# Two-layer RG-LRU and RWKV-7 decoder trunk on one core: a chunked scan with 64x64 products on all four quarters of the PE array, and smaller edits around it

## The chip, the core and the metric

The kernel runs on one core of a Trainium2 chip. The core has a matrix engine (TensorE, PE in the profile; PEld is its loading of stationary operands), a vector engine (VectorE, DVE), a scalar engine (ScalarE, ACT), a general engine (GpSimd, POOL) and a queue that issues most transfers (SyncE, SP). Each engine works through its own list of instructions in order and waits on semaphores for the others. The metric is the device time of one execution in microseconds (us).

## The reference, cut to what matters

The trunk has two layers on 1024 tokens of width 1024. Each layer is a token mixer (layer 0: RG-LRU; layer 1: RWKV-7), a cross-attention with 4 heads into 256 memory tokens, and a squared-ReLU MLP of width 4096. Every part is wrapped in two RMS norms, `x = x + rms_norm(f(rms_norm(x, g0)), g1)`. The part that the change rewrites is the recurrence of RWKV-7, for 16 heads of 64 channels:

```python
def step(state, inp):                     # state: 16 heads of 64 x 64
    r_t, w_t, k_t, v_t, a_t, b_t = inp
    sa = jnp.einsum('bhij,bhj->bhi', state, a_t)
    state = (state * w_t[:, :, None, :] + sa[..., None] * b_t[:, :, None, :]
             + v_t[..., None] * k_t[:, :, None, :])
    y_t = jnp.einsum('bhij,bhj->bhi', state, r_t)
    return state, y_t
_, ys = lax.scan(step, state0, seq_inputs)   # 1024 steps
```

Behind it each head's output is normalised over its 64 channels (mean and variance), scaled, shifted and gated.

## The kernel before

All large products run as three passes (`mm3`, lines 318 to 320): each 32-bit operand is split into a rounded part and a rest (`split`, line 233 on ACT and 234 on DVE). A recording pass lists all weight tiles, and a second pass loads and splits them ahead of use. The framework's scheduler may reorder instructions; `self.line(name)` keeps everything inside it in program order on each engine, and `self.behind()` keeps what it holds behind all that was issued.

**The scan** (lines 1657 to 1870) is cut into 16 chunks of 64 tokens; chunk c needs the state that chunk c-1 left. The 16 heads are 8 pairs (index q) of two heads (h), one on partitions 0 to 63 and one on 64 to 127 (`hr[h]`). Within a chunk, in the names of the code:

- `scan_gram(c, g)` (L1685): for half g of the heads, products of the chunk's keys `st` with its queries and removal vectors `mv`; `scan_mask` (L1695, DVE) masks them into `gw`, and ACT copies a block of `mv` beside it (L1697).
- `values(m)` (L1796): `gw` times the tile `sv`, which holds the state and the chunk's values; ACT copies the result (L1798). `from_state(m)` (L1808) is the state's share of the output. `solved(m)` (L1814) applies a triangular inverse; DVE scales the result and writes it into `sv` over the state (L1816).
- `decayed(m)` (L1803, POOL): the state times the chunk's total decay. It reads the state in `sv`, so L1816 of the same chunk has to wait for it.
- `scan_scale` (L1674, POOL) multiplies the keys with the chunk's decay; `scan_keys` (L1709, PE) transposes them, ACT copies them to `gk` (L1710).
- `update(m)` (L1821): `gk` times `sv`; DVE adds the decayed state (L1823), which is the state of the next chunk. `output()` (L1828) completes the chunk's output, which ACT copies (L1830).
- `post_var(c)` (L1721 on ACT: eight squares with sums; L1723 and L1724 on POOL: scale, then the power -1/2), `post_norm(c)` (L1729, DVE) and `flip_out(c)` (L1736 on PE, L1741 on DVE, L1742 on POOL) normalise, transpose and gate an earlier chunk's output.

The list `todo` sets the order of these in a chunk, all of it inside `self.line("scan")`. In chunk c the grams, masks, scaled and transposed keys of chunk c+1 are made. Before, `todo` reads: decayed, scan_scale(c+1), values and from_state by halves, **post_var(c-1)**, solved, flip_out(c-2), scan_gram(c+1, 0), update, scan_keys(c+1), scan_mask, scan_gram, scan_mask, output, post_norm(c-1). The loads of two chunks (`load`, L1630 for `st`, L1633 for `mv`) are issued on SP one pair of chunks ahead.

**Around the scan**: `tail` normalises the result of each part tile by tile (128 tokens): sum of squares on ACT (L327), scale and power on POOL (L329, L331), then on DVE result x norm x gain (L677) and + x (L678). `tphase` is the product before it, with the split of its first tile ahead of it. `xattn` goes through (head, half) steps: scores, softmax, transposes, values. `mlp` streams the up projection's results through memory, and its down projection begins with `block(0)`, `weights(0)`, `block(1)`.

## Time and profile before

| | |
|---|---|
| runs (3) | median 2851.32 us, 2850.32 to 2852.19 |
| profiled execution | 2850.88 us, span 2849.2 us, granted PE clock 0.993 |
| PE busy | 97% of the span |
| DVE, ACT, POOL busy | 65%, 50%, 32% |
| scan, chunks 2 to 14 (first product to first product of chunk 15) | 1764.38 to 1892.24 us |

The profile gives busy time by engine, groups of instructions by source line, waits with what ended them, and a timeline. In a timeline row the columns are start (us), length (us), engine, line, operation, output<-input tiles with their kinds (u, z: on-chip tiles, q, p: matmul banks, s, g: small columns, d: memory), shapes, and the count; a bracket gives the engine's idle time before the row and what ended it. A product of plain 32-bit operands is two PE instructions in the trace, a transpose one. Rows merge instructions that follow each other; a row's length runs to the end of the last one, which overlaps the next row's start.

### The profile page before, as it was taken

The numbers are of one execution on the slowest core, as the hardware profiler recorded it, in microseconds if no ns is written. First come the engines' busy times: TensorE is split into PE (matmuls) and PEld (weight loads), VectorE is DVE, ScalarE is ACT, GpSimd is POOL, SyncE is SP. The second block draws the span as 40 slices with busy tenths as digits, with TensorE's granted clock in tenths as the row PEclk, the third lists the DMA queues.
The fourth block names the chain that finished last, engine by engine and source line by source line (L and its number), as shares of the span: only waits on it lengthen the run. The fifth ranks groups of instructions, "written<-read, shape, count | busy, mean of one in ns | idle before, by whom it ended". The sixth has DMA issues, their size and how long they took to land.

```text
span 2849.2 us, 42748 instructions
## 1 busy us (share of the span) xinstructions
PE 2770.1 (97%) x16955; PEld 2312.1 (81%) x16955; DVE 1855.0 (65%) x2016; ACT 1424.0 (50%) x2191; POOL 912.2 (32%) x962
## 2 busy tenths in 40 slices
PE   7999999999999999999999999999999999999998
PEld 6888788888888888887777788888888888888886
DVE  5477557557454577888685835775665645567778
ACT  5456345545545544337672544654563644455333
POOL 2000114013666510003088223853203376640001
PEclk9999999999999999999999999999999999999999
DMA  8212342323454564424557799962222345464453
GB/s 264 74 45 77 101 165 83 104 82 100 152 161 148 204 211 155 155 89 134 171 150 225 215 252 241 240 155 96 78 86 97 99 160 159 148 240 162 149 176 118
DMA packets 383912, 421.92 MB, mean 148 GB/s; under 512 B 91504, under 2 KB 294496, under 8 KB 383712
## 3 DMA queue, kind: packets, MB, share of 16 engines
q1 hardware_dynamic: 371680, 379.19, 44.1%
q0 software_dynamic: 11568, 39.41, 3.8%
q8 instruction: 133, 2.18, 0.3%
q14 instruction: 67, 0.55, 0.1%
q10 hardware_dynamic: 464, 0.59, 0.1%
HBM read 283.79 MB, written 134.74 MB: 147 GB/s over the span
## 4 chain that ended last, share of the span: by engine, by line
PE 80%; POOL 5%; DVE 4%; DMA 3%; issue 3%; ACT 3%; SPq 2%; POOLq 0%; DVEq 0%; ACTq 0%
PE q L318 17%; PE q L320 17%; PE q L319 17%; PE p L318 7%; PE p L320 7%; PE p L319 7%; DMA u<-d 2%; POOL u L1434 2%; POOL w L1432 2%; PE q L1685 1%; ACT u L233 1%; DVE u L234 1%; POOL s L331 1%; PE q L1808 1%; DMA u<-in_b_w_rkv 1%
## 5 line engine op out<-in xcount | busy, mean ns | idle before, releaser
L234 DVE TENSOR_TENSOR u<-u,u 128x1024 fp32r<-128x1024 f32 (+1 forms) x602 | 808.5, 1374 | 351.7 <-ACT u L233 327.9
L233 ACT CAST u<-u 128x1024 fp32r<-128x1024 f32 (+1 forms) x602 | 591.5, 1019 | 443.0 <-DVE u L1064 224.6
L318 PE MATMUL q<-u,u 128*128 128x512 f32 (+1 forms) x1952 | 744.1, 383 | 5.7 <-ACT u L233 2.4
L319 PE MATMUL q<-u,u 128*128 128x512 f32 (+1 forms) x1952 | 745.6, 382 | 0.0
L320 PE MATMUL q<-u,u 128*128 128x512 f32 (+1 forms) x1952 | 740.6, 382 | 0.8 <-DVE u L234 0.8
L318 PE MATMUL p<-u,u 128*128 128x512 f32 (+1 forms) x1472 | 555.1, 379 | 17.3 <-ACT u L233 7.2
L320 PE MATMUL p<-u,u 128*128 128x512 f32 (+1 forms) x1472 | 552.4, 375 | 4.9 <-DVE u L234 4.9
L319 PE MATMUL p<-u,u 128*128 128x512 f32 (+1 forms) x1472 | 553.1, 376 | 2.4 <-DVE u L234 2.3
L329 POOL TENSOR_SCALAR s<-s 128x1 f32<-128x1 f32 x98 | 40.8, 417 | 1268.3 <-ACT u L327 1266.6
L318 PEld LDWEIGHTS q<-u,u 128*128 128x128 f32 x1952 | 367.0, 188 | 78.5 <-ACT u L233 3.5
L320 PEld LDWEIGHTS q<-u,u 128*128 128x128 f32 x1952 | 366.8, 188 | 72.1 <-DVE u L234 1.0
L319 PEld LDWEIGHTS q<-u,u 128*128 128x128 f32 x1952 | 367.1, 188 | 70.3 <-DVE u L234 0.3
L318 PEld LDWEIGHTS p<-u,u 128*128 128x128 f32 x1472 | 280.8, 191 | 70.5 <-ACT u L233 12.8
L320 PEld LDWEIGHTS p<-u,u 128*128 128x128 f32 x1472 | 280.9, 191 | 56.9 <-DVE u L234 7.5
L319 PEld LDWEIGHTS p<-u,u 128*128 128x128 f32 x1472 | 281.2, 191 | 52.8 <-DVE u L234 5.0
L444 POOL TENSOR_TENSOR u<-u,u 128x512 f32<-128x512 f32 x120 | 186.1, 1556 | 8.9 <-PE q L319 5.1
L1122 DVE TENSOR_TENSOR z<-z,q 128x512 f32<-128x512 f32 x192 | 130.5, 683 | 80.9 <-PE q L320 80.9
L318 PE MATMUL q<-z,u 128*128 128x512 f32 x320 | 124.9, 390 | 1.6 <-ACT u L233 1.6
L319 PE MATMUL q<-z,u 128*128 128x512 f32 x320 | 124.5, 389 | 0.0
L320 PE MATMUL q<-z,u 128*128 128x512 f32 x320 | 124.2, 389 | 0.0
L445 POOL TENSOR_TENSOR u<-u 128x512 f32<-128x512 f32 x40 | 75.9, 1897 | 145.4 <-DVE u L234 73.1
L1019 POOL TENSOR_TENSOR u<-u,u 128x512 f32<-128x512 f32 x32 | 46.0, 1436 | 176.6 <-ACT u L1008 166.7
(251 smaller groups left out, 3317.2 us busy)
## 6 DMA issues: line engine op xcount, KB each, us to landing
u<-d SPq DMA_DIRECT2D x194, 512.0 KB, 4.8
d<-u SPq DMA_DIRECT2D x109, 512.0 KB, 3.3
d<-u POOLq DMA_DIRECT2D x68, 512.0 KB, 3.3
d<-u SPq DMA_DIRECT2D x132, 256.0 KB, 3.4
u<-in_m_w_up SPq DMA_DIRECT2D x64, 512.0 KB, 5.4
u<-in_m_w_down SPq DMA_DIRECT2D x64, 512.0 KB, 7.5
u<-in_c_w_kv SPq DMA_DIRECT2D x32, 512.0 KB, 6.5
u<-in_b_w_rkv SPq DMA_DIRECT2D x24, 512.0 KB, 6.6
```

What stands on the lines that cost most here:

```text
L233: self.nc.scalar.copy(hv, src)
L234: (eng or self.nc.vector).tensor_tensor(lv, src, hv, ALU.subtract)
L318: mm(o, ah, bh, start=first, stop=False, **kw)
L319: mm(o, ah, bl, start=False, stop=False, **kw)
L320: mm(o, al, bh, start=False, stop=last, **kw)
L329: nc.gpsimd.tensor_scalar(v, ss, 1.0 / n, eps, ALU.mult, ALU.add)
L444: sub = lambda o, x, y: nc.gpsimd.tensor_tensor(o, x, y, ALU.subtract)
L445: nc.gpsimd.tensor_tensor(s[:, a], f1[:, a], f1[:, b], ALU.add)
L1019: tt(s1, r21, r22, ALU.add)
L1122: nc.vector.tensor_add(to_, to_, o)
L1432: eng.tensor_tensor(tv, xv_[:, 0:n, s:s + 1].broadcast_to([128, n, m]), Lv[:, s:s + 1, s + 1:].broadcast_to([128, n, m]), ALU.mult)
L1434: eng.tensor_tensor(xv_[:, 0:n, s + 1:], xv_[:, 0:n, s + 1:], tv, ALU.add)
```

## The change

In the scan, `scan_gram`, `from_state`, `solved` and the keys are written as products on 64 x 64 quarters of the array that go round all four quarters (`quads`, `tile_position`), with the heads of the upper half of q stored swapped. The keys are no longer scaled by POOL and transposed; POOL makes a diagonal tile (identity x decay, one 128x512 instruction for two), and one product with it scales and transposes at once. `st` is loaded in runs of 128 tokens for 64. The output bank is one per half of the heads. `todo` has a new order, in which `post_var(c-1)` is last in the chunk and `post_norm` is one chunk later. Outside the scan: `tail` multiplies result and gain ahead of the norm and joins the rest in one DVE instruction; the last tile's norm has fewer POOL steps; `tphase` can split its first tile in two cuts and does so behind RG-LRU; the last GELU is in two halves; `xattn` has another order of its steps, loads an activation table earlier and moves the held sums; `mlp` issues `block(1)` later.

```diff
-    def tphase(self, rows, z, post, mid=None):
+    def tphase(self, rows, z, post, mid=None, cuts=1):
 
         zs = {}
 
         def zsplit(tt):
             if tt < 8:
-                zs[tt] = self.split(z(tt), view=lambda t: t.rearrange("p (k t) -> p k t", t=128))
+                zs[tt] = self.unit(F32R), self.unit(F32R)
+                n = KT // (1 if tt else cuts)
+                for k in range(0, KT, n):
+                    self.split(z(tt)[:, k:k + n], *zs[tt], view=lambda t: t.rearrange("p (k t) -> p k t", t=128)[:, k:k + n])
 
...
-        def first(tt, src, ss):
+        def first(tt, src, r):
+            if r is None:
+                r = self.rstd(src, self.unit())
             o = self.unit()
-            r = self.rstd(src, o, ss=ss)
+            for s in (slice(512, 1024), slice(0, 512)) if last and tt >= HALVES else (slice(0, 1024),):
+                nc.vector.tensor_mul(o[:, s], src[:, s], gb[:, s])
             for n in range(1 + FETCH[last]):
                 fetch(tt + n)
             x = held[tt]
@@ -669,13 +674,10 @@
 
                     for n in range(2):
                         s = slice(n * 512, n * 512 + 512)
-                        y = self.unit()
-                        nc.vector.scalar_tensor_tensor(y[:, s], src[:, s], r, gb[:, s], ALU.mult, ALU.mult)
-                        nc.vector.tensor_add(y[:, s], y[:, s], x[:, s])
-                        (nc.sync, nc.scalar)[n].dma_start(xdst[tt * 128:tt * 128 + 128, s], y[:, s])
+                        nc.vector.scalar_tensor_tensor(o[:, s], o[:, s], r, x[:, s], ALU.mult, ALU.add)
+                        (nc.sync, nc.scalar)[n].dma_start(xdst[tt * 128:tt * 128 + 128, s], o[:, s])
                     return
-                nc.vector.scalar_tensor_tensor(o, src, r, gb, ALU.mult, ALU.mult)
-                nc.vector.tensor_add(x, o, x)
+                nc.vector.scalar_tensor_tensor(x, o, r, x, ALU.mult, ALU.add)
...
+            nc.scalar.activation(self.small(1), self.nhalf[:, :1], AF.Exp)
+            held, self.held = self.held, None
+            with self.behind(), self.line("held"):
...
-        steps = [(hd, hf) for hd in range(4) for hf in range(2)]
+        steps = [(0, 0), (0, 1), (1, 0), (1, 1), (2, 0), (3, 0), (2, 1), (3, 1)]
...
             block(0)
             weights(0)
+
+        def first():
             block(1)
-
-        def first():
             for work in parts(0):
...
-                        nc.gpsimd.tensor_tensor(sq[0], sq[0], sq[1], ALU.add)
-                        post(7, acc[1][:, 3, :], sq[0])
+                        nc.gpsimd.tensor_scalar(sq[0], sq[1], 1.0 / D, sq[0], ALU.mult, ALU.add)
+                        nc.gpsimd.tensor_tensor(sq[1], sq[0], self.nhalf[:, :1], ALU.pow)
+                        post(7, acc[1][:, 3, :], sq[1])
...
-            st = self.unit().rearrange("p (e q w t) -> p e q w t", e=2, q=4, w=2)
-            for e in range(2):
-                es = slice(n * 128 + e * 64, n * 128 + e * 64 + 64)
-                nc.sync.dma_start(st[:, e], STd[:, 4 * g:4 * g + 4, :, es])
+            st = self.unit().rearrange("p (q w t) -> p q w t", q=4, w=2)
+            nc.sync.dma_start(st, STd[:, 4 * g:4 * g + 4, :, ts])
...
+    quads = [(0, 0), (1, 1), (0, 1), (1, 0)]
+
     def scan_scale(c):
 
         if c >= 15:
             return
         s = cst[c]
-        s["sc"] = self.unit()
-        scv = s["sc"].rearrange("p (q w t) -> p q w t", q=8, w=2)
-        for g in range(2):
-            qs = slice(4 * g, 4 * g + 4)
-            nc.gpsimd.tensor_tensor(scv[:, qs], s["st"][g], s["pcc"][:, qs].unsqueeze(3).broadcast_to([128, 4, 2, 64]), ALU.mult)
+        s["sc"] = self.unit()[:, 0:512].rearrange("p (q i) -> p q i", i=64)
+        nc.gpsimd.tensor_tensor(s["sc"], self.id64.unsqueeze(1).broadcast_to([128, 8, 64]),
+                                s["pcc"].broadcast_to([128, 8, 64]), ALU.mult)
 
...
-            for h in range(2):
+            for h, w in quads:
                 with self.line("gram"):
-                    mm(s["pv", g][h][:, q, :], s["st"][g][hr[h], q].rearrange("p w t -> p (w t)"), s["mv"][hr[h], 4 * g + q],
-                       start=True, stop=True)
+                    mm(s["pv", g][h][hr[w], q, :], s["st"][g][hr[h], q, w, :], s["mv"][hr[h], 4 * g + q],
+                       start=True, stop=True, tile_position=(h * 64, w * 64))
 
...
+        s["gk"] = self.unit().rearrange("p (q h i) -> p q h i", q=8, h=2)
+        tps = [self.bank(h).rearrange("p (q i) -> p q i", i=64) for h in range(2)]
+        for q in range(8):
+            for h, w in quads:
+                mm(tps[h][hr[w], q, :], s["st"][q // 4][hr[h], q % 4, w, :], s["sc"][hr[h], q, :],
+                   start=True, stop=True, tile_position=(h * 64, w * 64))
+        for h in range(2):
+            nc.scalar.copy(s["gk"][:, :, h, :], tps[h])
...
+        def from_state():
+            Y.extend(self.bank(m)[:, 0:256].rearrange("p (q i) -> p q i", i=64) for m in range(2))
+            for q in range(4):
+                for h, m in quads:
+                    mm(Y[m][hr[h ^ m], q, :], mv[hr[h], m * 4 + q, 1, :], sv[hr[h], m * 4 + q, h, :],
+                       start=q == 0, stop=False, tile_position=(h * 64, (h ^ m) * 64))
+
+        def solved():
+            for q in range(4):
+                for h, m in quads:
+                    r = h ^ m
+                    mm(U[m][hr[h], q, :], xtc[hr[r], m * 4 + q, :], wsb[m][hr[r], q, :], start=True, stop=True,
+                       tile_position=(r * 64, h * 64))
+            for m in range(2):
+                qs = slice(m * 4, m * 4 + 4)
+                for h in range(2):
+                    nc.vector.tensor_tensor(sv[hr[h], qs, h, :], U[m][hr[h]], dbv[hr[h], qs].broadcast_to([64, 4, 64]), ALU.mult)
 
...
+        more = c and c < 15
         todo = [(decayed, 0), (decayed, 1)] if c < 15 else []
-        if c:
+        if more:
             todo += [(scan_scale, c + 1)]
-        todo += [(values, 0), (from_state, 0), (values, 1), (from_state, 1)]
-        if c:
-            todo += [(post_var, c - 1)]
-        todo += [(solved, 0), (solved, 1)]
+        todo += [(values, 0), (values, 1), (from_state,)]
+        if more:
+            todo += [(scan_gram, c + 1, 0)]
+        todo += [(solved,)]
+        if more:
+            todo += [(scan_keys, c + 1)]
+        if c < 15:
+            todo += [(update, 0), (update, 1)]
+        if more:
+            todo += [(scan_mask, c + 1, 0), (scan_gram, c + 1, 1)]
+        todo += [(output,)]
+        if c > 1:
+            todo += [(post_norm, c - 2)]
+        if more:
+            todo += [(scan_mask, c + 1, 1)]
         if c > 1:
             todo += [(flip_out, c - 2)]
         if c:
-            todo += [(scan_gram, c + 1, 0)]
-        if c < 15:
-            todo += [(update, 0), (update, 1)]
-        if c:
-            todo += [(scan_keys, c + 1, 0), (scan_keys, c + 1, 1), (scan_mask, c + 1, 0), (scan_gram, c + 1, 1), (scan_mask, c + 1, 1)]
-        todo += [(output,)]
-        if c:
-            todo += [(post_norm, c - 1)]
+            todo += [(post_var, c - 1)]
...
```

In the listings of the built programs that follow, names are output<-inputs, with buffer numbers: u and g are on-chip tiles, z the queries and removal vectors, pc the decays, id the 64 x 64 identity. First POOL in the scan before, one chunk from its decayed states on (L1803: decayed, L1674: scaled keys, L1723 and L1724: variance and power of chunk c-1, L1742: gate of an earlier chunk), and the start of the next:

```order
L1803 TENSOR_TENSOR u_16077<-u_16083,pc 64x256 x4
L1674 TENSOR_TENSOR u_16614<-u_16422,pc 128x512
L1674 TENSOR_TENSOR u_16614<-u_16425,pc 128x512
L1723 TENSOR_SCALAR g_16653<-g_16653 128x8
L1724 TENSOR_TENSOR g_16653<-g_16653,nhalf 128x8
L1742 TENSOR_TENSOR u_16524<-u_16524,u_15734 128x8x64
L1803 TENSOR_TENSOR u_16430<-u_16433,pc 64x256 x4
```

The same place on POOL now (L1818: decayed, L1688: the diagonal, L1759: gate, L1740 and L1741: variance and power of chunk c-1):

```order
L1818 TENSOR_TENSOR u_15249<-u_15255,pc 64x256 x4
L1688 TENSOR_TENSOR u_15906<-id_8762,pc 128x512
L1759 TENSOR_TENSOR u_15887<-u_15887,u_14829 128x8x64
L1740 TENSOR_SCALAR g_16095<-g_16095 128x8
L1741 TENSOR_TENSOR g_16095<-g_16095,nhalf 128x8
L1818 TENSOR_TENSOR u_15682<-u_15685,pc 64x256 x4
```

Variance and power stood between the scaled keys and the gate; now they stand behind the gate, directly ahead of the next chunk's decayed states.

ACT in the scan before, one chunk from the copies of `values` on (L1798), with the squares of chunk c-1 (L1721), the copies of the keys (L1710), those beside the masks (L1697) and that of the output (L1830):

```order
L1798 COPY u_15549<-q_15558 128x256
L1798 COPY u_15549<-q_15576 128x256
L1721 ACTIVATE u_15384,g_15594<-u_15384 128x64 x8
L1710 COPY u_15662<-q_15663 128x512
L1710 COPY u_15662<-q_15669 128x512
L1697 COPY u_15675<-z_13697 64x4x64 x2
L1697 COPY u_15690<-z_13697 64x4x64 x2
L1830 COPY u_15549<-q_15550 128x512
L1798 COPY u_15737<-q_15746 128x256
```

ACT now (L1813: values, L1727: keys, L1712: beside the masks, L1850: the output by halves, L1738: squares of chunk c-1):

```order
L1813 COPY u_15901<-q_15908 128x256
L1813 COPY u_15901<-q_15918 128x256
L1727 COPY u_15984<-q_15985 128x8x64
L1727 COPY u_15984<-q_15986 128x8x64
L1712 COPY u_16041<-z_13731 64x4x64 x2
L1850 COPY u_15901<-q_15928 128x256
L1850 COPY u_15901<-q_15929 128x256
L1712 COPY u_16083<-z_13731 64x4x64 x2
L1738 ACTIVATE u_15695,g_16095<-u_15695 128x64 x8
L1813 COPY u_16128<-q_16135 128x256
L1813 COPY u_16128<-q_16145 128x256
```

The squares stood right behind the copies of `values`; now they stand behind the last copy that follows the masks, ahead of the next chunk's copies of `values`.

DVE in the scan before, from the scaling of `solved` (L1816) on: gate product of an earlier chunk (L1741), the sums that make the next state (L1823), masks (L1695), norm (L1729):

```order
L1816 TENSOR_TENSOR u_15021<-q_15393,db 64x256 x2
L1816 TENSOR_TENSOR u_15021<-q_15411,db 64x256 x2
L1741 TENSOR_TENSOR u_15465<-q_15460,u_14677 128x8x64
L1823 TENSOR_TENSOR u_15024<-u_15018,q_15393 64x256 x2
L1823 TENSOR_TENSOR u_15024<-u_15018,q_15411 64x256 x2
L1695 TENSOR_TENSOR u_15511<-q_15468,mask 128x4x128
L1695 TENSOR_TENSOR u_15511<-q_15469,mask 128x4x128
L1695 TENSOR_TENSOR u_15526<-q_15516,mask 128x4x128
L1695 TENSOR_TENSOR u_15526<-q_15517,mask 128x4x128
L1729 TENSOR_TENSOR u_15196<-u_15196,g_15429 128x512
```

DVE now (L1837: scaling, L1844: sums, L1710: masks, L1746: norm, L1758: gate product):

```order
L1837 TENSOR_TENSOR u_15255<-q_15918,db 64x256
L1837 TENSOR_TENSOR u_15255<-q_15908,db 64x256 x2
L1837 TENSOR_TENSOR u_15255<-q_15918,db 64x256
L1844 TENSOR_TENSOR u_15685<-u_15249,q_15908 64x256 x2
L1844 TENSOR_TENSOR u_15685<-u_15249,q_15918 64x256 x2
L1710 TENSOR_TENSOR u_16041<-q_15946,mask 128x4x128
L1710 TENSOR_TENSOR u_16041<-q_15947,mask 128x4x128
L1746 TENSOR_TENSOR u_15468<-u_15468,g_15890 128x512
L1710 TENSOR_TENSOR u_16083<-q_16046,mask 128x4x128
L1710 TENSOR_TENSOR u_16083<-q_16047,mask 128x4x128
```

The gate product moved from between scaling and sums to the chunk's end, and the norm from behind the four masks to between them.

76 lines of the change are left out of this document (33 added, 43 removed).

## The prediction

> **What bounds the kernel now.** I read the page first: busy shares and the chain that ended last.
>
> ```profile
> span 2849.2 us, 42748 instructions
> ...
> PE 2770.1 (97%) x16955; PEld 2312.1 (81%) x16955; DVE 1855.0 (65%) x2016; ACT 1424.0 (50%) x2191; POOL 912.2 (32%) x962
> ...
> PE 80%; POOL 5%; DVE 4%; DMA 3%; issue 3%; ACT 3%; SPq 2%; POOLq 0%; DVEq 0%; ACTq 0%
> ```
>
> PE is busy for 97% of the span and carries 80% of the chain. So an edit pays where it shortens PE's own work or one of the few waits in front of PE, and costs where it makes PE wait. Most of the diff lies in the scan, so I asked for the busy time of each engine between the first `values` product of chunk 2 and that of chunk 15, which is 13 chunks.
>
> ```profile
> core 0: us, PE busy (x) PEld busy (x) DVE busy (x) ACT busy (x) POOL busy (x), PEclk, DMA share, GB/s
> 1764.38:1892.24 127.86, 125.55 (x2644) 111.85 (x2644) 93.73 (x181) 74.94 (x320) 95.80 (x110) 0.99 0.97 223
> ```
>
> A chunk takes 127.86 / 13 = 9.84 us, with PE busy 98% and the transfers' engines 0.97 (the column before the last). POOL is busy 75% of it, DVE 73%. The timeline of one chunk shows how that closes:
>
> ```profile
> 1809.69 1.15 PE L1821 MATMUL q<-u,u 128*64 128x64 f32 x32
> 1810.42 1.77 DVE L1823 TENSOR_TENSOR u<-u,q 64x256 f32<-64x256 f32 x4 [0.15 <-PE q L1821]
> ...
> 1810.77 1.09 PE L1709 MATMUL q<-ident,u 128*128 128x128 f32 x8
> ...
> 1811.80 1.16 PE L1685 MATMUL q<-z,u 64*128 64x128 f32 x16
> 1812.22 2.66 POOL L1803 TENSOR_TENSOR u<-u,pc 64x256 f32<-64x256 f32 x4
> 1812.22 2.48 DVE L1695 TENSOR_TENSOR u<-q,mask 128x512 f32<-128x512 f32 x4
> ...
> 1814.63 0.80 DVE L1729 TENSOR_TENSOR u<-u,g 128x512 f32<-128x512 f32 x1
> 1814.74 0.40 ACT L1697 COPY u<-z 64x256 f32<-64x256 f32 x1 [0.19 <-DVE u L1695]
> 1814.95 2.37 POOL L1674 TENSOR_TENSOR u<-u,pc 128x512 f32<-128x512 f32 x2
> ...
> 1815.65 0.68 ACT L1798 COPY u<-q 128x256 f32<-128x256 f32 x2
> ...
> 1815.84 0.68 PE L1808 MATMUL q<-u,z 64*64 64x64 f32 x16
> ...
> 1816.35 0.26 ACT L1721 ACTIVATE u<-u 128x64 f32<-128x64 f32 x1
> 1816.35 1.33 PE L1814 MATMUL q<-u,u 64*64 64x64 f32 x32
> ...
> 1817.13 1.78 DVE L1816 TENSOR_TENSOR u<-q,db 64x256 f32<-64x256 f32 x4 [1.70 <-PE q L1814]
> ...
> 1818.18 0.19 ACT L1721 ACTIVATION_READ_ACCUMULATOR u<-u 128x1 f32 x1
> ...
> 1818.45 0.20 POOL L1723 TENSOR_SCALAR g<-g 128x8 f32<-128x8 f32 x1 [1.13 <-ACT u L1721]
> 1818.73 1.65 POOL L1724 TENSOR_TENSOR g<-g,nhalf 128x8 f32<-128x8 f32 x1
> ...
> 1820.35 1.28 POOL L1742 TENSOR_TENSOR u<-u,u 128x512 f32<-128x512 f32 x1
> ```
>
> Three things are to be seen. PE goes from one block to the next. The decayed states (POOL L1803) start at 1812.22, as soon as the sums that make the state end (DVE L1823, 1810.42 + 1.77 = 1812.19). And the squares of an earlier chunk (ACT L1721), its variance and its power (POOL L1723, L1724: 1818.45 to 1820.35) run while PE does other work; before the next state is ready only the gate (L1742) follows them on POOL. In these rows nobody waits for POOL.
>
> **The scan, step by step.** *PE's own work.* 32 instructions that use two quarters at a time take 1.08 us (L1821 starts 1809.69, the next block 1810.77), 34 ns each. What four quarters give is shown by the gram products of an earlier stage, of the same 64x64x64 shape, which already go round all four:
>
> ```profile
> 1381.68 1.16 PE L1403 MATMUL q<-u,u 64*64 64x64 f32 x64
> 1382.78 0.96 PE L1333 MATMUL q<-u,u 64*128 64x512 f32 x6
> ```
>
> 64 instructions in 1.10 us, 17.2 ns each. So `from_state` and `solved`, 32 instructions each, fall from 34 to 17.2 ns: -1.08 us a chunk. The keys become 64 instructions, 1.10 us, in place of 8 transposes, 1.03 us (1810.77 to 1811.80): +0.07. The gram stays: twice the instructions at half the time. PE would save 1.0 us a chunk. The Trainium skill (TensorEngine Tiling (Array Packing), Instruction Overhead) gives each matmul some 60 cycles of overhead, which at the 2.4 GHz of its front page (Trainium Kernel Development and Optimization, NeuronCore Architecture) is 25 ns, an estimate; read as a floor of one instruction it would make the keys 1.6 us and the forecast 6 us longer. The 17.2 ns are against that reading.
>
> *The order.* This decides. In the listings `post_var(c-1)` is now the last item of a chunk, on ACT behind the copies that follow the last masks, on POOL directly ahead of the next chunk's decayed states. Each engine works in order, so these states now wait for the power, the power for the squares, the squares for the masks, and the masks for the state. On the other side, L1837 may not overwrite the state before it was read, and the keys' product waits for the diagonal, which POOL makes behind the decayed states, while `update` stands behind the keys on PE. That closes a loop from one state to the next, and each of its parts has a row above:
>
> - two masks, norm, two masks on DVE: from 1812.22 to the end of L1729, 1815.43: 3.2 us;
> - the last copy beside a mask, from the last mask's end (1814.70) to 1815.14: 0.45;
> - eight squares and their sums, from 1816.35 until POOL starts on them at 1818.45: 2.1;
> - variance and power, until the next POOL instruction can start at 1820.35: 1.9;
> - four decayed states, 1812.22 to the scaling's start at 1814.95: 2.73;
> - the diagonal: one instruction of 128x512 for L1674's two, half of 2.37: 1.2. Both operands are now repeated along an axis, which no row shows; I bound it by one 64x256 instruction (2.66 / 4 = 0.67) and by both old ones (2.37), and take 1.2, as the size is the same;
> - PE's wait on POOL, 0.1 (an estimate from DVE's 0.15 on PE in the row of 1810.42), and the keys, 1.1 (bounds: 1.03 as now, 2.2 if only two quarters overlap);
> - `update` to the end of the sums, 1809.69 to 1812.19: 2.5.
>
> The sum is 15.3 us for a chunk, against 9.84. What could be longer lies inside: DVE's scaling of `solved` (1.78) waits for the third decayed state only, some 2 us after the first starts, and ends before the keys do; the copies of `values` (0.68) and `solved` run beside the power and the decayed states; `flip_out` runs beside the squares; grams and `output` fit into PE's idle time. The transfers have 5 us more per chunk, and fewer packets, as each run of `st` is twice as long.
>
> *How often.* `decayed` of chunk c stands behind `post_var` from chunk 2 on, to chunk 14. So the loop runs from the `update` of chunk 1 to that of chunk 14:
>
> ```profile
> 1757.92 1.17 PE L1821 MATMUL q<-u,u 128*64 128x64 f32 x32
> ...
> 1888.48 1.15 PE L1821 MATMUL q<-u,u 128*64 128x64 f32 x32
> ...
> 1897.53 2.04 PE L1828 MATMUL q<-u,u 128*64 128x64 f32 x32
> 1899.50 0.50 PE L318 MATMUL p<-u,u 128*128 128x512 f32 x1
> ```
>
> Before, that is 1888.48 - 1757.92 = 130.6 us. Now it is 12 x 15.3 and, for chunk 14, which makes no keys (no diagonal; `update` follows the scaling), 15.3 less 1.2, 1.1 and 0.1 and plus about 1.0 that the scaling then sticks out: 13.9; together 197.5. That is +66.9. Behind it, from the `update` of chunk 14 to the next product phase: before 1899.50 - 1888.48 = 11.0; now 2.5 + 3.2 + 0.45 + 2.0 (squares ahead of the copies of `values`) + 0.7 + 0.7 (`solved`) + 1.9 + 1.1 (`output`) = 12.6: +1.6. Chunks 0 and 1 may save 1 us each on PE; I count nothing there. Scan: **+68.5 us**. Bounds of the loop: 14.5 with the short diagonal, 17.6 with the long one and the keys by halves.
>
> **Outside the scan** PE's waits are the price list (the bracket is the idle time before the row):
>
> ```profile
> 304.35 0.50 PE L318 MATMUL p<-u,u 128*128 128x512 f32 x1 [3.06 <-ACT u L233]
> ...
> 532.28 1.28 ACT L952 ACT_TABLE_LOAD   x1 [1.86 <-DVE s L947]
> ...
> 535.56 0.39 PE L318 MATMUL p<-u,u 128*128 128x256 f32 x1 [2.07 <-ACT u L952]
> ...
> 579.03 1.14 PE L964 MATMUL q<-ident,u 128*128 128x128 f32 x8 [1.37 <-ACT z L977]
> ...
> 685.54 1.64 PE L390 MATMUL q<-ident,u 128*128 128x128 f32 x13 [0.66 <-DVE u L685]
> ...
> 965.75 0.50 PE L318 MATMUL q<-u,u 128*128 128x512 f32 x1 [1.18 <-ACT u L233]
> ...
> 2839.94 0.29 POOL L1132 TENSOR_TENSOR s<-s,s 128x1 f32<-128x1 f32 x1 [1.08 <-ACT u L1131]
> ...
> 2840.32 0.58 POOL L329 TENSOR_SCALAR s<-s 128x1 f32<-128x1 f32 x1
> ...
> 2842.62 0.68 DVE L674 TENSOR_TENSOR u<-u,u 128x512 f32<-128x512 f32 x1
> ...
> 2843.88 1.89 DVE L674 TENSOR_TENSOR u<-u,u 128x512 f32<-128x512 f32 x3
> ```
>
> RG-LRU's output product waits 3.06 for the split behind the last GELU; with two cuts the first half needs older tiles only: -2.5 (bounds -3.1 and 0). The scores wait 2.07, in which ACT loads a table for 1.28; loaded earlier: -1.3 (0 to -2.1). The new order of steps may remove waits such as the 1.37 or make others: -1 (+3 to -4). At three seams the transposes wait some 0.66 for a norm that loses one DVE instruction of about 1.2: -1.8 (0 to -2.0). The MLP's first cast waits 1.18 in each of two layers, and the later `block(1)` may free it a tile: -1.2 (0 to -2.4). At the end the four DVE instructions from 1841.95 on lose two of 0.6 to 0.7, and POOL's first two become one (0.29): -1.6 (-0.7 to -2.2). The moved sums of the attention: 0 (1.5 either way). Together **-9.4**, from +3.8 to -17.3 if all went one way.
>
> **The sum.** The profiled execution took 2850.88 us, 0.44 under the median of the runs (2851.32). 2850.88 + 68.5 - 9.4 = **2910 us**, 2% slower.
>
> **Rivals.**
>
> *PE stays the bound (faster).* If the loop took less than PE's work, a chunk would fall by the 1.0 us above: 13 x 1.0 and 9.4 less, 2828 us. For it speaks that PE is 98% busy now. By the Trainium skill (TensorEngine Tiling (Array Packing), Theoretical Speedup) a side of 64 or less gains up to twice in PE's throughput, which is this rival's mechanism. Against it: the loop would have to lose over 6 us, more than squares, variance and power together (4.0), and its links stand in program order. It decides only below about 8.8 us a loop. Chance 0.07.
>
> *The loop closes one step earlier.* If the diagonal of the next chunk were ready when `update` comes, the loop would end over the scaling, as in chunk 14: 13.9 for 15.3, so 2910 - 12 x 1.4 = 2893. The listing speaks against it: the diagonal stands behind the decayed states. Chance 0.12.
>
> *The quarters do not overlap* with operands cut out of longer rows: keys 2.2, +1.1 in the loop, 2910 + 13 = 2923. The gram would double too, but in PE's idle time. The 17.2 ns row speaks against it. Chance 0.1.
>
> *The edits outside the scan carry and the loop is hidden in part*, so that both cancel to within 0.2% (5.7 us, about what this measurement can tell from no change): the loop would be near 10.5 us. Chance 0.02.
>
> **Numbers.** The forecast has 0.69. The range reaches from 2880 (the shorter loop of the second rival with 13 us more saved outside or in shorter POOL instructions) to 2936 (the long diagonal, 12 x 1.2 = 14, and half of the keys' 13, with nothing saved outside beyond 4). Slower by over 0.2%: 0.91; within 0.2%: 0.02; faster: 0.07.
>
> **What would show it.** In the scan the starts of `update` 15.3 us apart; PE busy some 57% there (8.7 of 15.3); PE's wait in front of the keys (L1724), ended by POOL (L1688), some 4 us long and once in a chunk; POOL's squares-variance-power-decayed-diagonal without a gap; DVE's scaling (L1837) released by POOL (L1818). `from_state`, `solved` and keys at 17 ns an instruction. Outside: no wait of 3 us at RG-LRU's output product, PE's busy time down by about 13 x 1.0. It is wrong if POOL's power no longer takes 1.65, if the chunk stays under 10 us, or if PE waits for something else in front of `update`.

## The result and the profile after

The changed kernel takes 2928.16 us (median, 2924.64 to 2930.18), the kernel before 2850.07 us in the same session: a ratio of 1.027, 95% interval 1.0258 to 1.0283. That is 78 us more; 59 were forecast, and 2928 lies in the range given (2880 to 2936). One execution each of experiments 9 and 10 below fell into a slower state of the chip (4983.6 and 3349.61 us) and is left out of every median here.

The page of the changed kernel, with the lines that answer to those of before:

```profile
span 2928.5 us, 45365 instructions
...
PE 2781.5 (95%) x18307; PEld 2319.6 (79%) x18307; DVE 1860.7 (64%) x2017; ACT 1423.1 (49%) x2210; POOL 893.8 (31%) x951
...
PE 27%; DVE 1%; ACT 1%; POOL 1%; issue 1%; DMA 0%; POOLq 0%; DVEq 0%; SPq 0%; ACTq 0%
```

PE has 1352 more matmuls and is busy 11 us longer, although two blocks of each chunk became shorter. The chain adds up to a third of the span: followed back from the end, it breaks off behind the scan and says nothing on it. So I went to the scan directly. Its starts of `update` split the difference between the two profiled executions into four stretches:

| stretch | before | after | difference |
|---|---|---|---|
| to the `update` of chunk 1 | 1757.92 | 1757.43 | -0.5 |
| from there to the `update` of chunk 14 | 130.56 | 210.57 | +80.0 |
| from there to the next product phase | 11.02 | 11.09 | +0.1 |
| the rest of the span | 949.7 | 949.4 | -0.3 |

The windows view of the eleven chunks in the middle (span and columns as in the prediction; the three numbers at the end are PE's clock, the share of the transfers' engines, GB/s):

```profile
1775.44:1953.68 178.24, 117.34 (x3217) 102.32 (x3213) 75.63 (x154) 64.71 (x286) 72.26 (x88) 0.83 0.53 133
```

A chunk takes 178.24 / 11 = 16.20 us, against 9.84. PE is busy 66% of it, no engine is full, and the transfers, 0.97 before, are at 0.53. So a chain of waits sets the time. The timeline shows one chunk, from keys to keys:

```profile
1821.99 1.99 PE L1724 MATMUL q<-u,u 64*64 64x64 f32 x64 [4.52 <-POOL u L1688]
1823.90 1.97 PE L1842 MATMUL q<-u,u 128*64 128x64 f32 x32
...
1825.07 1.75 DVE L1844 TENSOR_TENSOR u<-u,q 64x256 f32<-64x256 f32 x4 [3.38 <-PE q L1842]
1825.81 1.93 PE L1700 MATMUL q<-z,u 64*64 64x128 f32 x32
1826.85 1.29 DVE L1710 TENSOR_TENSOR u<-q,mask 128x512 f32<-128x512 f32 x2
...
1828.06 0.68 DVE L1746 TENSOR_TENSOR u<-u,g 128x512 f32<-128x512 f32 x1
...
1828.66 1.28 DVE L1710 TENSOR_TENSOR u<-q,mask 128x512 f32<-128x512 f32 x2
...
1829.97 0.40 ACT L1712 COPY u<-z 64x256 f32<-64x256 f32 x1 [0.19 <-DVE u L1710]
...
1832.51 0.20 POOL L1740 TENSOR_SCALAR g<-g 128x8 f32<-128x8 f32 x1 [0.62 <-ACT u L1738]
...
1832.79 1.65 POOL L1741 TENSOR_TENSOR g<-g,nhalf 128x8 f32<-128x8 f32 x1
1834.40 2.63 POOL L1818 TENSOR_TENSOR u<-u,pc 64x256 f32<-64x256 f32 x4
1836.38 1.53 DVE L1837 TENSOR_TENSOR u<-q,db 64x256 f32<-64x256 f32 x4 [5.84 <-POOL u L1818]
1837.11 1.04 POOL L1688 TENSOR_TENSOR u<-id,pc 128x512 f32<-128x512 f32 x1
1838.21 1.99 PE L1724 MATMUL q<-u,u 64*64 64x64 f32 x64 [4.52 <-POOL u L1688]
```

Read it as a ring. The sums (L1844) make the state at 1826.82. The masks and the norm end at 1829.94 and the last copy beside a mask at 1830.37. ACT's eight squares end as POOL takes the variance at 1832.51, POOL's power ends at 1834.4, the decayed states at 1837.0, the diagonal at 1838.15, and only then may the keys start. Of the brackets, 4.52 us is PE's wait, once a chunk, and 5.84 is DVE's for the third decayed state. That was forecast, link by link.

One thing was not: the rows of PE just behind its wait. From the start of the keys to that of `update` are 1.91 us, from there to the gram 1.91, and the gram takes 1.86; 1.1, 1.08 and 1.09 were expected. The windows of those microseconds show why:

```profile
1822.00:1824.00 2.00, 2.00 (x66) 1.88 (x68) 0.00 (x0) 0.00 (x0) 0.00 (x0) 0.50 1.15 245
1824.00:1826.00 2.00, 2.00 (x36) 1.88 (x40) 0.88 (x3) 1.07 (x2) 0.00 (x0) 0.50 1.16 290
1826.00:1828.00 2.00, 2.00 (x42) 1.72 (x41) 1.94 (x4) 0.41 (x1) 0.00 (x0) 0.61 1.14 273
1828.00:1830.00 2.00, 1.94 (x50) 1.66 (x46) 2.00 (x5) 1.48 (x5) 0.00 (x0) 1.00 0.65 178
```

The granted clock (third number from the end) is 0.50 for 5.6 us from the start of these keys on (0.61 in the third window is 0.50 up to 1827.56), and then 1.00 again. Behind the waits of the other chunks in the window it is 0.50 for 3.0 to 5.6 us.

### The profile page after: what moved, and what is told of

It reads as the page before. It is cut to its first block, busy times and chain, and to the rows that moved or that the text cites. A ratio compares the mean times of both kernels' runs of the same rounds, so it can differ in the third digit from the quotient of the medians.

```text
span 2928.5 us, 45365 instructions
## 1 busy us (share of the span) xinstructions
PE 2781.5 (95%) x18307; PEld 2319.6 (79%) x18307; DVE 1860.7 (64%) x2017; ACT 1423.1 (49%) x2210; POOL 893.8 (31%) x951
## 5 line engine op out<-in xcount | busy, mean ns | idle before, releaser
L318 PEld LDWEIGHTS p<-u,u 128*128 128x128 f32 x1472 | 281.0, 191 | 68.6 <-ACT u L233 12.9
L444 POOL TENSOR_TENSOR u<-u 128x512 f32<-128x512 f32 x40 | 68.2, 1705 | 147.8 <-DVE u L234 102.8
```

Of the source, the lines that this page charges most:

```text
L318: mm(o, ah, bh, start=first, stop=False, **kw)
L444: nc.gpsimd.tensor_tensor(s[:, a], f1[:, a], f1[:, b], ALU.add)
```

## The experiments

The theory: the place of `post_var(c-1)` at the end of a chunk closes the ring, and the halved clock makes it a little longer. The main rivals: the new products, the diagonal or the keys ahead of `update` are dear by themselves; the edits outside the scan give less than forecast.

**1. The squares, variance and power back in their place** (changed kernel):

```
-        todo += [(post_var, c - 1)]          # last in the chunk
+        todo += [(post_var, c - 1)]          # behind from_state
```

> The changed kernel with one item moved: the squares, variance and power of the chunk before stand again behind from_state, where they were. Theory (the place of this item closes a loop over ACT and POOL): POOL then goes straight from the sums to decayed and diagonal, 2.6 + 1.0 us, so the keys wait about 1 us in place of 4.5, a chunk falls from 16.2 to between 8.8 (PE's work) and 9.8 us, and the clock is not halved any more: 2840 us, 2828 to 2850, nearly all of the 78 us gone. Rival (the four-quarter products or the diagonal are dear by themselves): a chunk of over 12 us and a time over 2870.

Measured: 2889.85 us, ratio to before 1.013 (1.0106 to 1.0154). Half of the loss goes, and not the whole. A chunk still takes 12.9 us. Its timeline names what stands ahead of the decayed states now:

```profile
1811.38 0.63 PE L1753 MATMUL q<-ident,u 128*128 128x128 f32 x4 [1.12 <-DVE u L1746]
...
1813.11 1.27 POOL L1759 TENSOR_TENSOR u<-u,u 128x512 f32<-128x512 f32 x1 [5.41 <-DVE u L1758]
...
1814.34 2.63 POOL L1818 TENSOR_TENSOR u<-u,pc 64x256 f32<-64x256 f32 x4
...
1818.15 1.50 PE L1724 MATMUL q<-u,u 64*64 64x64 f32 x64 [2.58 <-POOL u L1688]
...
1819.58 1.97 PE L1842 MATMUL q<-u,u 128*64 128x64 f32 x32
```

PE's flip (L1753) waits for the norm (L1746), which stands between the masks. POOL waits 5.41 us for the product behind the flip (L1758), makes the gate (L1759), and only then the decayed states. The flip was moved to the chunk's end as well. So there are two rings, one of 15 us over the power (16.2 with the halved clock) and one of 13 over the gate; I had priced the longer and called the flip covered.

**2. The order alone, on the kernel before:**

```
-        if c: todo += [(post_var, c - 1)]                   # behind from_state
-        if c > 1: todo += [(flip_out, c - 2)]
+        if c > 1: todo += [(post_norm, c - 2), (flip_out, c - 2)]
...
-        if c: todo += [(post_norm, c - 1)]                  # last in the chunk
+        if c: todo += [(post_var, c - 1)]
```

> The kernel before, with only this order changed: the squares, variance and power last in a chunk, the norm and the flip of the chunk before that behind solved (one chunk later than before). Products, transposed keys and the scaling of the keys stay. Theory: the loop closes here too, but over DVE's scaling of solved in place of the keys, as these stand behind the update: sums 2.5, masks 2.5, last copy 0.45, squares 2.1, variance and power 1.9, two decayed states 1.4, scaling 1.2 to 1.8, then PE: about 12.3 us for a chunk in place of 9.84, so 12 x 2.5 = 30 us more, 2880 us (2865 to 2900). Rival (the order costs only together with the keys ahead of the update): under 2857.

Measured: 2957.6 us, 1.0372 (1.0356 to 1.0387): with the products of before this order costs 106 us, more than the whole change. The direction is as expected, the size is a miss, and two rows of its timeline say why:

```profile
1825.99 1.12 PE L1736 MATMUL q<-ident,u 128*128 128x128 f32 x4 [4.91 <-DVE u L1729]
...
1829.05 1.97 PE L1821 MATMUL q<-u,u 128*64 128x64 f32 x32
```

I had put the norm (L1729) behind DVE's scaling, which waits for the decayed states, and the flip (L1736), on PE, ahead of the `update` (L1821). Norm, flip and gram are links of this ring too, 18 us in all, and the `update` of 1.97 us stands in a halved clock here as well. So this kernel shows that an order without any new product can cost this much; it does not isolate the power.

**3. POOL's two instructions moved, ACT's squares left last** (changed kernel):

```
+        if c > 1: todo += [(post_pow, c - 2)]     # variance, power: behind decayed and diagonal
```

> The changed kernel, with only POOL's variance and power taken out of the place: they stand behind the next chunk's decayed states and diagonal; the eight squares stay last on ACT. This tells whether POOL alone closes the loop or ACT as well. Theory with both: the loop then closes over ACT, as the copies of values stand behind the squares: sums 2.5, masks and norm 3.2, last copy 0.45, squares 2.1, copies of values 0.7, solved 0.6, its scaling 1.3, and update 1.1 where the keys are done by then: 11 to 12 us for a chunk, 2875 us (2860 to 2890). Rival (POOL alone): as with the whole item moved, 2828 to 2850.

Measured: 2891.87 us, 1.0145 (1.0128 to 1.0162), neither of the two cases. In the chunks quoted a turn takes 13.7 us, and again it is the gate that POOL waits for, 6.67 us, right ahead of the decayed states:

```profile
1830.39 1.27 POOL L1762 TENSOR_TENSOR u<-u,u 128x512 f32<-128x512 f32 x1 [6.67 <-DVE u L1761]
...
1831.62 2.63 POOL L1821 TENSOR_TENSOR u<-u,pc 64x256 f32<-64x256 f32 x4
```

A test that moves one of two rings cannot tell what the other hides: whether the squares alone would close one at 11 to 12 us cannot be seen behind the gate.

**4. All items in the order of before, with the new products:**

```
+        todo, in short: decayed, scan_scale, values 0 and 1, from_state, post_var(c-1), solved, flip_out(c-2),
+              gram 0, update, keys, mask 0, gram 1, mask 1, output, post_norm(c-1)
```

> The changed kernel with all items of a chunk in the order of the kernel before (squares, variance, power behind from_state; flip and gate behind solved; keys behind update; norm last): the four-quarter products, the diagonal and the edits outside stay. With the item of squares and power alone moved back the time stayed at 2890: there the decayed states start behind POOL's gate (L1759), the gate behind the flip, the flip behind the norm between the masks. Theory (a chunk is closed by what stands on POOL ahead of the next decayed states, power or gate): with both back POOL is free at the state, a chunk takes 9 to 9.9 us, 2840 to 2850 in all. Rival (the keys through the diagonal or the new products cost by themselves): over 2870.

Measured: 2867.92 us, 1.0048 (1.0035 to 1.006). The order explains 60 of the 78 us. But this time the rival was nearly right: 15 us above before, and 28 above the kernel of experiment 5, stay with the products. The waits of PE between 1764 and 1884 us (in total, times, longest) are no longer for POOL:

```profile
PE q L1849 <- issue: 4.6, 1, 4.6
PE q L1724 <- issue: 4.0, 3, 3.0
PE q L1753 <- issue: 3.5, 1, 3.5
PE q L1700 <- issue: 2.8, 3, 1.3
PE q L1842 <- issue: 2.0, 2, 1.1
PE q L1832 <- issue: 1.8, 1, 1.8
PE q L1811 <- issue: 1.5, 2, 1.3
```

"issue" is time in which PE waited for nothing the profile shows: 20.2 us of 120, in the middle of blocks too (what these waits are is shown in the last section). In the kernel before it is 0.8 there, in that of experiment 5 4.4. A chunk now has 292 PE instructions (32 each for `values`, `from_state`, `solved`, `update` and `output`, 64 each for gram and keys, 4 transposes) in place of 204. Of the 28 us, 13.4 are in the loop by the profiled executions (148.05 from the `update` of chunk 1 to that of chunk 14, 134.62 in experiment 5), and 10.8 ahead of it.

**5. The edits outside the scan's block alone** (all of the diff up to the scan's block, the kernel before from there on):

> The kernel before with the edits outside the mixing stage of the scan's block alone (tails, RG-LRU, attention, MLP); the scan's products, keys and order stay. The prediction gave these edits -9.4 us (-17.3 to +3.8). PE's rows of the changed kernel show the wait at RG-LRU's output product shorter by 1.2 us only and other waits grown by some tenths each: so -3 us, 2844 to 2851, is expected now. Rival (the -9.4 holds and the scan alone is dearer than thought): 2838 to 2843.

Measured: 2839.52 us, 0.9956 (0.9942 to 0.9969), the fastest kernel of this study: 13 us less by the medians, 9 to 17 by the interval. The revised -3 was wrong, the forecast's -9.4 near. I had read the -3 from the waits of the changed kernel's profile, in which less of the gain is to be seen (experiments 11 and 12 come back to it). The scan's edits thus cost 78 + 13 = 91 us.

**6. Keys by transposes again, order of before** (236 PE instructions a chunk; POOL scales the keys again, two instructions in place of the diagonal's one):

```
-                mm(tps[h][hr[w], q, :], st[...], s["sc"][hr[h], q, :], tile_position=(h * 64, w * 64))    # 64
+            nc.tensor.transpose(tp[:, q], s["sc"][:, ...128 columns...], self.ident)                      # 8
```

> The changed kernel with the items of a chunk in the order before (as in the run of all items, 2868 us) and the keys made as before: 8 transposes of the scaled keys in place of 64 products with a diagonal, so 236 PE instructions a chunk in place of 292 (before: 204). In the run of all items PE stood 20 us of 120 in the scan waiting for nothing but its own instructions (issue), 5 us in the kernel with the edits outside alone. Theory (short instructions on four quarters use up PE's instruction stream faster than it is loaded): a good half of these 15 us goes, 2858 us (2853 to 2862). Rival (the waits do not depend on the number of instructions): 2866 to 2871.

Measured: 2855.01 us, 1.0013 (1.0003 to 1.0023): 13 us less than in experiment 4 by the medians, 10 by the ratios to the kernel before, with 56 instructions fewer a chunk. In the same window PE's issue waits sum to 12.9 us (20.2 in experiment 4). From the `update` of chunk 1 to that of chunk 14 the issue waits fall from 24.5 to 12.8 us, and that stretch from 148.05 to 139.89 us. So the keys through the diagonal cost more than the 0.07 us a chunk that their length says: 8.2 us in the loop, less than the issue waits that go; the rest I cannot place.

**7. Only `from_state` and `solved` on four quarters**, loads, gram and keys of before (204 instructions), norm early, masks around `output`:

> Of the scan's new products only from_state and solved go round the four quarters; loads, gram and keys are those of before, so PE has 204 instructions a chunk as before. The order is a new one: POOL free at the state, norm early, flip behind the gram, update, then keys, masks around the output. Theory: few issue waits, PE's work 1.0 us a chunk less than before, but the chunk stays bound by links of 8.9 to 9.4 us; with the 13 us from outside the scan 2833 to 2843 us. Rival (the parts ahead of the scan that the new layout needs cost what the scan gains): 2845 or more.

Measured: 2843.35 us, 0.9971 (0.996 to 0.9982); issue waits 2.4 us of 120. This is faster than before and not faster than experiment 5: the gain of 1.0 us a chunk in PE's work does not appear in the time. Its transfers' engines are busy 0.98 in the scan, PE waits 5.9 us for transfers in the loop (2.4 in experiment 5), and its `update` of chunk 1 starts 4.5 us later.

**8. All new products in a better order** (diagonal ahead of the decayed states, norm early, `update` ahead of the keys):

> All products of the changed kernel, 292 PE instructions a chunk, with the diagonal ahead of the decayed states on POOL and the norm early, update ahead of the keys, masks around the output. Without waits for instructions the links would give 8.8 us a chunk, 2843 us. Theory (issue waits of some 1.5 us a chunk stay, and grow as PE has less time): 2850 to 2862. Rival (the order alone was wrong, instructions come in time): under 2846.

Measured: 2861.75 us, 1.004 (1.0027 to 1.0052), at the upper end of what the theory gave. Issue waits of 22.7 us in the window eat what the order gives. Its own turns show it: of the thirteen from the `update` of chunk 1 to that of chunk 14, the four in which PE meets no issue wait take 8.8 to 9.2 us, as the links gave (9.4 to 9.8 in most turns of the kernel before), the other nine 9.7 to 16.8.

**9. and 10. The clock.** First 192 short products in PE's wait (9), then three wide ones (10), whose edit is this:

```
+            for n in range(3):
+                mm(tps[n % 2], self.ident, s["st"][n % 2], start=True, stop=True)     # then the keys overwrite it
```

> The changed kernel with 192 products more a chunk (3.3 us at 17.2 ns), put ahead of the keys' product into the same bank and overwritten by it: they fill most of PE's 4.5 us wait with work that nobody uses. Theory (the halved clock behind that wait lengthens keys and update): the granted clock stays near 1.0, the keys take 1.1 in place of 1.9 us and the update 1.1 in place of 1.9, so a chunk is 1.6 us shorter although PE does more: 2928 - 12 x 1.6 = 2909 us (2902 to 2916). Rival (the keys are slow by themselves, whatever the clock): keys still 1.9 us, 2925 to 2935.

> The changed kernel with three wide products (128x512, f32, about 1 us each, an estimate from 128x128 ones of 0.13 us) ahead of the keys' product in place of the 192 short ones tried before, which made PE wait for instructions: three instructions fill most of PE's 4.5 us wait, and their results are overwritten. Theory (the halved clock behind that wait lengthens keys, update and gram): granted clock near 1.0, keys and update 1.1 us each in place of 1.9, a chunk of 14.6 in place of 16.2 us, 2928 - 12 x 1.6 = 2909 us (2902 to 2916). Rival (the products are slow by themselves): 2925 or more.

Measured with 192 short ones: 2946.57 us, 1.0331 (1.0314 to 1.0349), slower, so it did not test the clock. What it showed came unasked: PE stood in issue waits in front of the short products themselves, up to 5.3 us at a time.

```profile
PE q L1726 <- issue: 17.5, 7, 5.3
PE q L1729 <- issue: 6.0, 3, 3.0
```

Measured with three wide ones: 2912.11 us, 1.0213 (1.0195 to 1.0232), 16 us less than the changed kernel although PE does more. Keys, `update` and gram behind the shorter wait in its timeline:

```profile
1834.78 1.16 PE L1727 MATMUL q<-u,u 64*64 64x64 f32 x64 [1.44 <-POOL u L1688]
1835.87 1.15 PE L1845 MATMUL q<-u,u 128*64 128x64 f32 x32
1836.95 1.32 PE L1700 MATMUL q<-z,u 64*64 64x128 f32 x32
```

And the window of its eleven chunks (columns as above):

```profile
1776.01:1940.66 164.65, 131.10 (x3284) 98.95 (x3279) 76.28 (x154) 64.64 (x286) 72.16 (x88) 1.00 0.57 144
```

Keys 1.09, `update` 1.08, clock 1.00, a chunk of 164.65 / 11 = 14.97 us. So the halved clock is 1.23 us of each turn, and the ring without it is 15.0.

**11. and 12. The loads.** Ahead of the scan the profiles differ by some 10 us, in places like this one of the changed kernel, where PE waits for DVE and DVE had waited for a transfer:

```profile
1691.83 1.28 DVE L1583 SCALAR_TENSOR_TENSOR u<-u,colt,u 128x1024 f32<-128x1024 f32 x1 [11.07 <-DMA u<-d]
...
1693.77 1.60 PE L1486 MATMUL q<-u 32*32 32x32 f32 x64 [2.54 <-DVE u L1612]
```

The changed kernel also writes the keys to memory in two stores for one, as the upper heads are swapped. Experiment 11 is the changed kernel with the short loads of before; 12 is the kernel of experiment 5 with the long loads and the gram on four quarters:

```
-            st = self.unit().rearrange("p (q w t) -> p q w t", q=4, w=2)
-            nc.sync.dma_start(st, STd[:, 4 * g:4 * g + 4, :, ts])
+            st = self.unit().rearrange("p (e q w t) -> p e q w t", e=2, q=4, w=2)
+            for e in range(2): nc.sync.dma_start(st[:, e], STd[:, 4 * g:4 * g + 4, :, es])      # 11; 12 is the reverse
```

> The changed kernel with one part undone: the keys of two chunks are loaded again in two transfers with runs half as long. Ahead of the scan, the update of chunk 1 started at 1745.3 us of the kernel with the edits outside alone, at 1749.8 with the two products and the old loads, at 1754 to 1758 in the kernels with the long loads; there PE waits 2.5 to 3.7 us at the last merge of the solve for a tile that DVE could not make before a transfer had landed. Theory (the long transfers hold up the small loads ahead of them): that update starts some 5 us earlier, and nothing changes inside the loop, which does not wait for transfers: 2923 us (2920 to 2926). Rival (not the loads but the stores in halves): 2926 to 2931. A gain by the long runs in the scan itself would show as more than 2931 here.

> The kernel with the edits outside alone (2839.5 us) with two parts of the scan's change added: the long loads, and the gram as 32 products over four quarters in place of 16 (220 PE instructions a chunk in place of 204); order, keys, scaling, from_state and solved as before. Theory (long loads hold up small ones ahead of the scan): update of chunk 1 some 5 us later than 1745.3, 2843 to 2848. Rival (fewer and longer transfers relieve the scan, where the transfers' engines are busy 0.92 to 0.98): 2832 to 2839, which would be the best kernel here.

Measured: 11 takes 2925.66 us, 1.0257 (1.0243 to 1.0271), not to be told from the changed kernel, and its `update` of chunk 1 starts at 1756.5 us, as late as before the edit. 12 takes 2853.77 us, 1.0013 (1.0004 to 1.0023): 14 us more than without its two parts, and its `update` starts at 1754.6. So neither the long loads (11 starts late without them) nor the stores in halves (12 has not got them) are needed for the late start, and loads and gram together cost more than they give (12).

All kernels with the gram on four quarters start that `update` 8.6 to 13.4 us later than experiment 5 in their profiled executions, the one with the old gram (7) 4.5. Not all of this is made by the scan's edits. The first gram product of the solve ahead of the scan (L1418 of the changed kernel) stands behind the same 6487 PE instructions in experiment 5 and in every kernel made from the changed one, and yet it starts between 1374.0 us (experiment 5) and 1378.9 (the changed kernel). Counted from there, the `update` of chunk 1 comes 371.3 to 376.2 us later in the four kernels with the old gram (before and experiments 2, 5, 7) and 378.1 to 383.1 in the others. Counted so, the merge behind the wait quoted above comes 3.9 us earlier in experiment 11 than in the changed kernel, as the wait falls from 11.1 to 7.5 us, but the next merge comes 2.8 us later. A part of the late start is issue waits: between the `update`s of chunks 0 and 1 the changed kernel takes 9.8 us, of which PE spends 3.0 in them, the kernel before 6.9 with none. What delays the rest stays open.

## Why the forecast held

**The place and the kind: right.** The time went into the scan, the ring closes as the listing said, PE waits once a chunk in front of the keys, ended by the diagonal, DVE's scaling is released by the decayed states, and POOL's chain from variance to diagonal has no gap.

**The loop: 15.3 forecast, 16.2 measured.** Term by term, from the timeline above: masks and norm 3.1 (3.2), last copy 0.43 (0.45), squares 2.14 (2.1), variance and power 1.89 (1.9), decayed states 2.71 (2.73), diagonal with PE's wait on it 1.10 (1.3), keys 1.91 (1.1), `update` to the end of the sums 2.92 (2.5). Six of eight are within 0.2. The step that failed in this sum is the price of the keys and of `update`: both were taken from rows at full clock, 17.2 and 34 ns an instruction, for work that stands behind a wait of over 4 us. Experiment 10 gives the sizes at full clock: 1.09 for the keys and 14.97 for the ring. The bounds of the diagonal were wide for nothing: 1.04 us, near the 1.2 taken. The lower bound of 14.5 for the loop should have been 14.8 by its own terms (15.3 less 1.2 and plus 0.67). The Trainium skill's overhead of an instruction (TensorEngine Tiling (Array Packing), Instruction Overhead), read as a floor, would have made the keys 1.6 us, an estimate; the 1.09 us at full clock decide against that reading.

**How often: right in number, two turns longer.** Eleven turns of 16.2, a first of 18.0 and a last of 14.3 make 210.6; 197.5 was forecast. Of the 13 us between them the eleven turns are 10, the first turn 2.7. The stretch behind, forecast at +1.6, came out at +0.1.

**Outside: -9.4 forecast, 13 less when made alone, next to nothing seen in the changed kernel.** The waits at RG-LRU's output product and at the scores fell, but not to nothing; in the changed kernel the first still reads

```profile
303.72 0.50 PE L318 MATMUL p<-u,u 128*128 128x512 f32 x1 [1.91 <-ACT u L233]
```

in place of 3.06. Two steps fail here. The sum is silent on the stages between these edits and the loop: I gave stores, loads and first grams there no term, and from the first gram product of the solve to the `update` of chunk 1 the changed kernel takes 7.3 us more than the one with the edits outside alone (378.6 for 371.3; 376.2 before). And it is silent on how far executions differ by themselves: another 4.9 us between these two (1757.4 for 1745.3 at that `update`, 12.2 in all) are there already at the solve's first gram, where their instructions are still the same.

**The misses add up, and the range held partly by luck.** The loop was 13 us too short and the gain outside, 9 us, is hardly seen; only the stretch behind the loop, 1.5 us too long, goes the other way. The median lies 18 us above the forecast. The range allowed 26, for a longer diagonal (14), for keys on half the quarters (6.5) and for less gain outside (5.4). The first two did not come; the halved clock, which the prediction does not name, took their room. Without it (experiment 10) the time is 2912, 2 us above the forecast, though the gain outside is hardly seen there either. Two of the marks named in advance did not hold: PE is busy 66% of a chunk and not 57%, as its instructions take longer at half clock, and its busy time went up and not down by 13.

**The rivals.** "The loop closes one step earlier" and "the quarters do not overlap" are out: the ring runs over the diagonal, and 64 keys take 1.09 us at full clock, 17 ns each. "PE stays the bound" gave 1.0 us a chunk to the new products once nothing else waits; experiments 4 and 8 take the other waits away and still end 15 and 11 us above the kernel before, since PE then waits for instructions (last section). That rival's premise, that PE's time is the sum of its blocks' lengths, does not hold either. That gains and losses cancel is out by the 78 us.

## What to carry to other kernels

Before a product is made shorter, follow the state of a recurrence through every engine's program order and add the links: an item that is put last on one engine can become first ahead of the next state, and when one such ring is undone, look at once for the next shorter one, which the same move may have made. Price work that stands behind a long wait of PE (2 us and more in these kernels) at half clock. And count instructions, not only their time: twice as many products at half the length were no gain here, since PE then waited for the instructions.

## What the runs showed that was not expected

**The clock.** Behind a wait of 4.5 us PE ran at 0.50 for 3.0 to 5.6 us. The Trainium skill has the rule (TensorE: Matmul & The Clock Gate, Part 1: the clock is halved after an idle window of some 3.4 us and comes back after as long a busy one), and the trace agrees with the length: in all fourteen traces the clock changes only at steps of 3.41 us. I had not applied it. It does not take a single wait of that length, though. With the power back in its place (experiment 1) PE waited 2.58 us and the clock was still halved behind five of eight such waits (`update` 1.91 us at 1819.58, quoted above). In experiment 3 waits of 1.8 to 2.0 us were followed by it eight times in ten, while with 1.4 to 1.8 us of wait in experiment 10 it stayed at 1.00. Where the wait falls between the steps decides in experiment 1: the wait from 1815.57 to 1818.15 lies inside one step (1815.37 to 1818.78) and the next step is halved; an equal one from 1803.16 to 1805.74 is cut in two by the step that ends at 1805.13, and no step is halved. How idle a step has to be does not come out sharply: in the fourteen traces no step with PE busy for more than 0.73 of it was followed by a change to the halved clock, and every full-clock step with less than 0.40 was.

**PE's instructions.** Rows of 64x64x64 products at 17 ns each made PE wait for `issue`: 0.8 to 4.4 us of 120 with 204 instructions a chunk, 10.2 with 220 (experiment 12), 12.9 with 236, 20.2 with 292, 22.7 in the denser order, and more still with 192 short ones in a row. That products go round four quarters does not make the waits by itself: experiment 7 has 64 such instructions a chunk and waits of 2.4 us. The trace has a queue of instruction loads beside these, 16 KB a piece; 19 pieces in this window of the kernel before and 24 in experiment 4. The waits are for these pieces: each of the 18 issue waits in the loop of experiment 4 ends 1.28 to 1.65 us after a piece has landed, while the pieces come 4.9 us apart in the mean, and all 106 issue waits in the loops of the fourteen traces end 1.24 to 1.74 us after one. Full transfer engines are not needed for it: the kernel with the 192 short products has the most, 43.5 us in its loop, with these engines busy 0.51. What limits the pieces was not tested. In the changed kernel itself the long turn hides most of it, 2.6 us in the window. The Trainium skill (Runtime: NRT & Kernel Launch, Instruction fetch mechanics) holds that such loading is hidden, as instructions are issued more slowly than they come; here, at 17 ns a product, these runs do not agree.
